# Moving the high and low slices of the activations 32 bytes apart by the remainder of 64

## The chip, the cores and the metric

The kernel runs on one core of a Trainium2 chip. The metric is the device time of one execution in microseconds; the time before is 1422.66 us, the median of three runs (1421.84 to 1422.71). A core has a matrix engine (TensorE, PE in the profile, with PEld for its weight loads), VectorE (DVE), ScalarE (ACT), GpSimd (POOL) and SyncE (SP), which work side by side and wait for each other by semaphores. On-chip memory (SBUF) has 128 partitions; an address in this text is the byte offset within a partition, the same in all of them. Matmul results land in PSUM.

## The reference, cut to what matters

The computation is a chain of transformer-like blocks on one sequence of 256 tokens and 1024 features, in float32.

```python
# first block
xn = rmsnorm(h, norm_mix_g)
q, k, v, xr, gr, ga, gb = split(xn @ w_in)
ya = chunked_band_attention(q, k, v, rel_table) @ w_attn_out
hr = rg_lru(causal_depthwise_conv(xr, conv_w, conv_b), ...)
yb = (hr * gelu(gr)) @ w_rnn_out
h = h + (sigmoid(ga + ...) * ya + sigmoid(gb + ...) * yb) @ w_o
h = h + (silu(g) * up) @ w_ffn_out          # g, up = split(rmsnorm(h) @ w_ffn_in)
x = rmsnorm(h, final_norm_g)
# second block, two layers: half-weighted feed-forward, mixer, half-weighted feed-forward
x = x + 0.5 * swiglu(rms_norm(x), w_in, w_out)      # four of these
x = x + chunked_sgu(h, ...)                          # layer 0: gated unit, v layer-normed
x = x + stick_breaking_attention(q, k_shared, v_shared) @ b_w_o   # layer 1
return rms_norm(x, final_norm)
```

Nearly all of the work is products of the 256 x 1024 activations with weight matrices.

## The kernel before, in words

The activations lie transposed: 128 features on the partitions, 256 tokens along the free dimension, so 1024 features are eight slices with k = 0 to 7. The weights come in as 240 groups of 1 MB (`PLAN`), each of two chunks of 128 x 1024. A chunk is of kind A (one block of 128 output features, all eight k: `pe_a`), K (two k, four output blocks: `pe_k`, or `pe_nat` where the activations are stationary and the weights move), or R (one k, eight output blocks: `pe_r`, and `pe_rn` with the weights moving).

For float32 accuracy each factor is split into a high part, rounded to the type fp32r, and a low part, the rest. `prep` does it for the weights (ScalarE line 163, VectorE line 164). A product is then three matmuls, `mm3` (line 213): weight high with activation high, weight high with activation low, weight low with activation high. The weight is the stationary operand (128 x 128), the activation slice the moving one: 256 columns of 4 bytes, so 1024 bytes per partition. All matmuls go through `mm` (line 211) in the order of the program; nothing reorders them.

The activation slices lie in two places. `self.XS` is a pair of tiles, `xh` and `xl`, of 128 x 8 x 256; it holds the normed input of each stage, written by `split_h` (ScalarE, line 262) and `split_l` (VectorE, line 267), one slice at a time. `self.RR` is four tiles of the same size for what comes between: RR[0] and RR[1] hold the high and low parts of the hidden activations (written by `hl_split`, lines 318 and 319), RR[2] and RR[3] those of the attention; in the gated unit the high parts fill RR[0] and RR[1] and the low ones RR[2] and RR[3].

Between the streams stand a few other matmuls: `stat_mm` sums squares (moving operand one column of `ones`); `bcast_mm` spreads the two columns of reciprocal norms `rc` (or `rckv`, for the keys and values, and `r1c`), stationary, against `ident`; `nudge` is one bf16 matmul of 32 columns on 64 partitions, with `identb` as both operands; the gate products of the recurrent part and those within the two attentions are plain fp32.

Constant tiles are laid one behind the other in the order of their declarations, each taking a multiple of 32 bytes. In `setup` the first is `par` (896 bytes, at 16512), then `x0` to `x3` (17408 on), `xh` (25600), `xl` (33792), `rr0` to `rr3` (41984, 50176, 58368, 66560), `sa`, six slabs, `ident`, `ones`. All of these start at a multiple of 64. The 8 bytes of `mhalf` (133248) put `rt`, `r1t`, `rkv` and `rckv` (136352) at remainder 32 of 64; `rc` is at 136448, remainder 0; `identb` (137696) at remainder 32.

Of the kernel before, what the change touches and what calls it, by code (L numbers as in the profile page):

```python
# [10 lines left out]
F32R = mybir.dt.float32r  # L11
# [90 lines left out]
for _n, _c in PARAMS:  # L102
    OFF[_n] = NPAR
    NPAR += _c


class Builder:
    def __init__(self, tc, dram, pools):
        self.tc, self.nc, self.dram = tc, tc.nc, dram
        self.cp, self.rawp, self.hlp, self.accp, self.wkp = pools  # L110
        self.ci = 0
        self.preps = 0
        self.loads = 0
        self.raw = {}
        self.hl = {}
        self.gens = []
        self.R = None
        self.rcol = None
        self.due = False
# [207 lines left out]
    def setup(self):  # L327
        nc, dram = self.nc, self.dram
        self.P = self.sb("par", [128, 224])[:, 0:NPAR]
        self.X = [self.sb(f"x{p}", [128, 2, 256]) for p in range(4)]  # L330
        self.XS = (self.sb("xh", [128, 8, 256], F32R), self.sb("xl", [128, 8, 256], F32R))
        self.RR = [self.sb(f"rr{i}", [128, 8, 256], F32R) for i in range(4)]
        self.SA = self.sb("sa", [128, 2080])[:, 0:8 * 259]
        self.SL = {c: self.sb("s" + c, [128, 2048]) for c in "bcdfgh"}
        self.ident = self.sb("ident", [128, 128])
        self.ones = self.sb("ones", [128, 128])
        self.mhalf = self.sb("mhalf", [128, 2])
        self.Rt = self.sb("rt", [128, 256])
        self.R1 = self.sb("r1t", [128, 256])
        self.Rkv = self.sb("rkv", [128, 256])  # L340
        self.rckv = self.sb("rckv", [128, 16])[:, 0:2]
        self.v2 = self.sb("v2", [128, 2])
        self.rc = self.sb("rc", [128, 2])
        self.tiny = self.sb("tiny", [128, 1])
        self.c8 = self.sb("c8", [128, 8])
        self.nc8 = self.sb("nc8", [128, 8])
        self.half = self.sb("half", [128, 24])
        self.sq = self.view("b", 4)
        nc.scalar.dma_start(self.P, dram["par"])
        x_load = lambda p: nc.sync.dma_start(self.X[p], dram["x"][:, 2 * p:2 * p + 2, :])  # L350
        for f in range(2):
            nc.sync.dma_start(self.X[0][:, f, :], dram["x"][:, f, :])  # L352
        self.warm_up()
        for g in range(2):
            t = self.rawp.tile([128, 2048], F32, tag="raw", name="raw")
            for c in range(2):
                if 2 * g + c:
                    x_load(2 * g + c)
                n = 512 if 2 * g + c == 0 else 1024
                for o in range(c * 1024, (c + 1) * 1024, n):  # L360
                    nc.sync.dma_start(t[:, o:o + n], dram["w"][g, :, o:o + n])  # L361
            self.raw[g] = t
        self.loads = 2
        self.load()
        self.gw = self.SL["h"].rearrange("p (a b) -> p a b", b=128)
        make_identity(nc, self.ident)
        nc.gpsimd.memset(self.ones, 1.0)
        nc.gpsimd.memset(self.mhalf, -0.5)
        nc.gpsimd.memset(self.tiny, 2.0 ** -115)
# [606 lines left out]
    def sgu(self, fin, fin_l):  # L976
# [6 lines left out]
        tmp = [SA[:, i * 512:(i + 1) * 512].rearrange("p (a b) -> p a b", b=256) for i in range(2)]  # L983
        rs = SL["b"][:, 0:1024]
        bs = SL["b"][:, 1024:2048]
        st6 = self.sb("bn6", [128, 2, 4, 6])
        mv = self.sb("mv", [128, 2, 2])
        rstd = self.sb("rstd", [128, 2])
        nc.gpsimd.dma_start(ws, dram["ws"])
        nc.gpsimd.affine_select(out=ws, in_=ws, pattern=[[0, 8], [1, 128]], compare_op=ALU.is_ge, fill=0.0,  # L990
                                base=0, channel_multiplier=-1)
# [367 lines left out]
```

## Time and profile before

| | before |
|---|---|
| median of three runs | 1422.66 us |
| profiled execution | 1422.0 us |
| its span, first to last instruction | 1420.3 us |
| granted TensorE clock, mean | 0.999 |
| TensorE matmuls, busy | 1410.6 us, 99% |
| TensorE weight loads, busy | 1368.7 us, 96% |
| VectorE, busy | 949.8 us, 67% |
| ScalarE, busy | 735.0 us, 52% |
| DMA | 260.31 MB, mean 183 GB/s |

A matmul's own duration in the profile (about 280 ns for 256 columns) is the time from its start to the modelled end of its results; matmuls overlap, so the distance between two starts is what adds up to the span. Weight loads run beside the matmuls in front of them.

### The profile page before, as it was taken

Reading aid. Unit: us, or ns where it says so; the run is one execution under the profiler, and the core shown is the slowest. Engines: PE = TensorE matmul, PEld = TensorE weight load, DVE = VectorE, ACT = ScalarE, POOL = GpSimd, SP = SyncE. Lnnn points to the kernel's source line nnn. Section 1 sums busy time; section 2 is a strip of 40 time slices with the busy share of each in tenths; the row PEclk is TensorE's granted clock in tenths of the full one; section 3 lists DMA queues with packets and bytes.
Section 4 is the critical chain, followed back from the end, with each engine's and each line's share of the span. In section 5 each row is a group of like instructions: output and inputs, shape, how many; then the busy total and the mean of one; then the engine's idle time right before and its main releaser. Section 6 shows DMA issues by size and latency. Waiting matters only on the chain.

```text
span 1420.3 us, 26991 instructions
## 1 busy us (share of the span) xinstructions
PE 1410.6 (99%) x11564; PEld 1368.7 (96%) x11564; DVE 949.8 (67%) x1316; ACT 735.0 (52%) x1094; POOL 24.7 (2%) x57
## 2 busy tenths in 40 slices
PE   9999999999999999999999999999999999999998
PEld 9998999999999999998999999999999998999997
DVE  6976687665567666677785665667665677656663
ACT  5686465544445445455445444446544477544442
POOL 0000000000000000000000000000000000000000
PEclk9999999999999999999999999999999999999999
DMA  8555554555544555556445554454555552445551
GB/s 299 192 198 197 176 189 154 203 195 191 179 178 149 206 182 206 203 198 223 160 156 183 186 206 179 178 188 169 208 184 211 199 179 90 161 152 197 190 187 51
DMA packets 37624, 260.31 MB, mean 183 GB/s; under 512 B 4224, under 2 KB 4608, under 8 KB 7040
## 3 DMA queue, kind: packets, MB, share of 16 engines
q1 hardware_dynamic: 36288, 253.77, 50.1%
q0 software_dynamic: 1072, 4.72, 1.0%
q8 instruction: 90, 1.47, 0.4%
q14 instruction: 30, 0.25, 0.1%
q10 hardware_dynamic: 144, 0.10, 0.0%
HBM read 257.53 MB, written 1.05 MB: 182 GB/s over the span
## 4 chain that ended last, share of the span: by engine, by line
PE 98%; DMA 0%; ACT 0%; DVE 0%; SPq 0%; issue 0%; POOLq 0%; POOL 0%
PE wk L211 62%; PE acc L211 36%; DMA raw<-w 0%; PE acc L530 0%; PE wk L530 0%; ACT sf L971 0%; ACT sd L961 0%; DVE l L164 0%; ACT h L163 0%; SPq L361 0%; SPq L352 0%; DVE sf L962 0%; POOLq L1355 0%; POOL rc L284 0%; ACT sh L1148 0%
## 5 line engine op out<-in xcount | busy, mean ns | idle before, releaser
L164 DVE TENSOR_TENSOR l<-raw,h 128x1024 fp32r<-128x1024 f32 (+1 forms) x479 | 571.3, 1220 | 241.3 <-ACT h L163 240.9
L211 PE MATMUL wk<-xh,h 128*128 128x256 f32 x2272 | 637.5, 281 | 1.4 <-ACT h L163 1.4
L211 PE MATMUL wk<-xh,l 128*128 128x256 f32 x2272 | 633.5, 279 | 0.1
L211 PE MATMUL wk<-xl,h 128*128 128x256 f32 x2272 | 633.2, 279 | 0.0
L163 ACT ACTIVATE h<-raw 128x1024 fp32r<-128x1024 f32 (+1 forms) x479 | 486.3, 1046 | 61.3 <-PE acc L211 28.0
L211 PEld LDWEIGHTS wk<-xh,h 128*128 128x128 f32 x2272 | 430.8, 190 | 4.5 <-issue 2.0
L211 PEld LDWEIGHTS wk<-xh,l 128*128 128x128 f32 x2272 | 427.7, 188 | 0.5 <-DVE l L164 0.5
L211 PEld LDWEIGHTS wk<-xl,h 128*128 128x128 f32 x2272 | 427.6, 188 | 0.5
L211 PE MATMUL acc<-rr,h 128*128 128x256 f32 x2016 | 353.5, 279 | 0.0
L211 PEld LDWEIGHTS acc<-rr,h 128*128 128x128 f32 x2016 | 306.1, 189 | 2.1 <-issue 1.9
L211 PE MATMUL acc<-rr,l 128*128 128x256 f32 x1008 | 280.4, 278 | 0.0
L211 PEld LDWEIGHTS acc<-rr,l 128*128 128x128 f32 x1008 | 189.3, 188 | 0.0
L748 ACT ACTIVATE sa<-sa 128x256 f32<-128x256 f32 x110 | 45.4, 417 | 258.5 <-DVE sa L315 258.3
L318 ACT ACTIVATE rr<-sa 128x256 fp32r<-128x256 f32 (+1 forms) x122 | 52.7, 439 | 185.3 <-DVE sa L753 128.9
L315 DVE TENSOR_TENSOR sa<-wk,rt 128x512 f32<-128x512 f32 x92 | 62.4, 687 | 72.5 <-PE wk L211 54.8
L319 DVE TENSOR_TENSOR rr<-sa,rr 128x256 fp32r<-128x256 f32 (+1 forms) x122 | 54.1, 451 | 53.4 <-ACT rr L318 53.4
L211 PE MATMUL acc<-h,rr 128*128 128x512 f32 (+1 forms) x208 | 63.1, 374 | 0.0
L211 PEld LDWEIGHTS acc<-h,rr 128*128 128x128 f32 x208 | 38.5, 188 | 6.6
L262 ACT ACTIVATE xh<-x,par 128x256 fp32r<-128x256 f32 x56 | 25.0, 501 | 29.4 <-DVE x L325 16.2
L211 PE MATMUL acc<-l,rr 128*128 128x512 f32 (+1 forms) x104 | 39.0, 375 | 0.0
L753 DVE TENSOR_TENSOR sa<-sa 128x256 f32<-128x256 f32 x88 | 37.1, 429 | 0.0
L211 PE MATMUL wk<-rr,h 128*128 128x256 f32 x192 | 33.0, 277 | 0.0
(255 smaller groups left out, 972.8 us busy)
## 6 DMA issues: line engine op xcount, KB each, us to landing
raw<-w SPq DMA_DIRECT2D x237, 1024.0 KB, 5.0
sd<-bias POOLq DMA_DIRECT2D x8, 384.0 KB, 3.4
raw<-w SPq DMA_DIRECT2D x3, 512.0 KB, 7.6
sh<-gates SPq DMA_DIRECT2D x1, 1024.0 KB, 9.1
out<-sf SPq DMA_DIRECT2D x4, 256.0 KB, 2.2
x<-x SPq DMA_DIRECT2D x3, 256.0 KB, 6.6
raw<-w SPq DMA_DIRECT2D x2, 256.0 KB, 4.9
sa<-ws POOLq DMA_DIRECT2D x1, 512.0 KB, 3.8
```

Of the source, the lines that this page charges most:

```text
L163: nc.scalar.activation(h[:, s], raw[:, s], AF.Copy)
L164: nc.vector.tensor_tensor(l[:, s], raw[:, s], h[:, s].bitcast(F32), op=ALU.subtract)
L211: self.nc.tensor.matmul(out, lhsT, rhs, start=start, stop=stop, skip_group_check=True)
L262: self.nc.scalar.activation(xs[0][:, k, :], src[p][:, f, :], AF.Copy, scale=self.par(*g(k)))
L315: self.nc.vector.tensor_tensor(dst, bank, self.Rpair(), op=ALU.mult)
L318: self.nc.scalar.activation(zh, src, AF.Copy)
L319: self.nc.vector.tensor_tensor(zl, src, zh.bitcast(F32), op=ALU.subtract)
L748: nc.scalar.activation(t[:, 0, :], t[:, 0, :], AF.Silu)
L753: nc.vector.tensor_tensor(t[:, 1, :], t[:, 0, :], t[:, 1, :], op=ALU.mult)
```

## The change: two tiles become four, and small tiles move between them

The two tiles `xh` and `xl` of eight slices are each cut into two tiles of four slices, one for even k and one for odd k. A small class, `Slices`, lets the code index them as before. Small constant tiles that stood further down (or in `sgu`) are declared between the large ones, so that the large ones behind them start 32 bytes off a multiple of 64 or on one again. By the declarations, the remainders of 64 after are: `xh0` 0, `xh1` 32, `xl0` 32, `xl1` 0; `rr0` 0, `rr1` 32, `rr2` 32, `rr3` 0. `rt`, `r1t`, `rkv`, `rckv` and `identb` come to remainder 0, `rc` stays at 0. The weights' tiles are not moved.

```diff
+class Slices:
+    def __init__(self, aps):
+        self.aps = aps
+    def __getitem__(self, i):
+        return self.aps[i[1]][i[0], i[2]]
...
-        self.XS = (self.sb("xh", [128, 8, 256], F32R), self.sb("xl", [128, 8, 256], F32R))
-        self.RR = [self.sb(f"rr{i}", [128, 8, 256], F32R) for i in range(4)]
+        quarter = lambda n: self.sb(n, [128, 4, 256], F32R)
+        xh0 = quarter("xh0")
+        self.rc = self.sb("rc", [128, 2])
+        xh1, xl0 = quarter("xh1"), quarter("xl0")
+        self.half = self.sb("half", [128, 24])
+        self.c8, self.nc8 = self.sb("c8", [128, 8]), self.sb("nc8", [128, 8])
+        self.mhalf = self.sb("mhalf", [128, 2])
+        self.v2 = self.sb("v2", [128, 2])
+        xl1 = quarter("xl1")
+        self.XS = tuple(Slices([t[k % 2][:, k // 2, :] for k in range(8)]) for t in ((xh0, xh1), (xl0, xl1)))
+        tile8 = lambda i: self.sb(f"rr{i}", [128, 8, 256], F32R)
+        self.RR = [tile8(0)]
+        self.tiny = self.sb("tiny", [128, 1])
+        self.RR += [tile8(1), tile8(2)]
+        self.bn6 = self.sb("bn6", [128, 2, 4, 6])
+        self.rstd = self.sb("rstd", [128, 2])
+        self.RR.append(tile8(3))
...
-        st6 = self.sb("bn6", [128, 2, 4, 6])
+        st6 = self.bn6
-        rstd = self.sb("rstd", [128, 2])
+        rstd = self.rstd
```

## Rows read from the trace of the kernel before

**Rows 1.** The page: span, busy time of each engine, granted clock in 40 slices.
```profile
span 1420.3 us, 26991 instructions
...
PE 1410.6 (99%) x11564; PEld 1368.7 (96%) x11564; DVE 949.8 (67%) x1316; ACT 735.0 (52%) x1094; POOL 24.7 (2%) x57
...
PEclk9999999999999999999999999999999999999999
```

**Rows 2.** The page: chain that ended last, by engine and by line.
```profile
PE 98%; DMA 0%; ACT 0%; DVE 0%; SPq 0%; issue 0%; POOLq 0%; POOL 0%
```

**Rows 3.** Groups of instructions: operands and count | busy us, mean ns | idle before.
```profile
L211 PE MATMUL wk<-xh,h 128*128 128x256 f32 x2272 | 637.5, 281 | 1.4 <-ACT h L163 1.4
L211 PE MATMUL wk<-xh,l 128*128 128x256 f32 x2272 | 633.5, 279 | 0.1
L211 PE MATMUL wk<-xl,h 128*128 128x256 f32 x2272 | 633.2, 279 | 0.0
L164 DVE TENSOR_TENSOR l<-raw,h 128x1024 fp32r<-128x1024 f32 (+1 forms) x479 | 571.3, 1220 | 241.3 <-ACT h L163 240.9
...
L211 PE MATMUL acc<-rr,h 128*128 128x256 f32 x2016 | 353.5, 279 | 0.0
...
L211 PE MATMUL acc<-rr,l 128*128 128x256 f32 x1008 | 280.4, 278 | 0.0
...
L319 DVE TENSOR_TENSOR rr<-sa,rr 128x256 fp32r<-128x256 f32 (+1 forms) x122 | 54.1, 451 | 53.4 <-ACT rr L318 53.4
...
L262 ACT ACTIVATE xh<-x,par 128x256 fp32r<-128x256 f32 x56 | 25.0, 501 | 29.4 <-DVE x L325 16.2 <-DVE x L323 12.1 <-DMA par<-par 1.1
L267 DVE SCALAR_TENSOR_TENSOR xl<-x,par,xh 128x256 fp32r<-128x256 f32 x56 | 23.8, 479 | 1.4 <-ACT xh L262 1.4
```

**Rows 4.** Chain that ended last, in order of time: start us, us, what.
```profile
274.24 5.76 PE wk L211 x48
280.56 8.69 PE wk L211 x72
...
842.47 11.31 PE wk L211 x96
...
975.67 5.76 PE wk L211 x48
981.99 8.38 PE wk L211 x72
...
1028.78 10.88 PE wk L211 x96
```

**Rows 5.** Windows, TensorE alone: window, length, busy (count), clock, DMA share, GB/s.
```profile
297.00:461.00 164.00, 164.00 (x1395) 1.00 0.50 180
809.00:975.00 166.00, 166.00 (x1412) 1.00 0.53 190
...
484.00:630.00 146.00, 146.00 (x1291) 1.00 0.59 212
...
997.00:1130.00 133.00, 133.00 (x1176) 1.00 0.56 197
...
108.00:126.00 18.00, 18.00 (x79) 1.00 0.52 177
```

**Rows 6.** Group of the gate matmuls (first line); timeline at 46 and 1277 us.
```profile
L211 PE MATMUL acc<-sb,sh 128*128 128x256 f32 x32 | 7.6, 379 | 0.0
...
46.45 1.89 PE L211 MATMUL acc<-sb,sh 128*128 128x256 f32 x8
...
1276.89 0.39 PE L211 MATMUL acc<-l,rr 128*128 128x512 f32 x1
1277.12 0.62 PE L211 MATMUL acc<-h,rr 128*128 128x512 f32 x2
1277.57 0.39 PE L211 MATMUL acc<-l,rr 128*128 128x512 f32 x1
```

**Rows 7.** Timeline of TensorE near 280 and 981 us: where the norms are spread.
```profile
279.83 0.61 PE L211 MATMUL acc<-ident,rc 128*128 128x128 f32 x4
280.37 0.19 PE L211 MATMUL acc<-identb 64*128 64x32 bf16 x1
...
981.26 0.61 PE L211 MATMUL acc<-ident,rckv 128*128 128x128 f32 x4
981.80 0.19 PE L211 MATMUL acc<-identb 64*128 64x32 bf16 x1
```

More of the change, by code (lines that the diff above doesn't have):

```diff
@@ L336, in setup @@
         self.ones = self.sb("ones", [128, 128])
-        self.mhalf = self.sb("mhalf", [128, 2])
         self.Rt = self.sb("rt", [128, 256])
@@ L341, in setup @@
         self.rckv = self.sb("rckv", [128, 16])[:, 0:2]
[L342 to L347, printed above, removed]
         self.sq = self.view("b", 4)
```

## The prediction

> **What bounds the kernel now.** I read the summary first. TensorE's matmuls cover 1410.6 of 1420.3 us with a granted clock of nine tenths or more in all 40 slices, while VectorE is busy 67% and ScalarE 52% [rows 1]. A busy TensorE may only be a pipelined one, so the chain of waits comes next: 98% of it is TensorE's own queue at line 211, DMA and the other engines together stay at a few tenths of a per cent [rows 2]. The table of waits and idle times agrees: the largest group of matmuls has 1.4 us of idle time before it, the others 0.1 or none [rows 3]. So the time is the number of matmuls times the distance from one start to the next, and only that distance matters.
>
> What is that distance? In the chain, a piece of 96 matmuls of 256 columns takes 11.31 us at 842.47 and 10.88 us at 1028.78 [rows 4]: 117.8 ns and 113.3 ns a step, for the same shapes and the same code. The windows, with a granted clock of 1.00 in each, show that this is no local noise: 297 to 461 us holds 1395 matmuls (117.6 ns each) and 809 to 975 holds 1412 (117.6), while 484 to 630 holds 1291 (113.1) and 997 to 1130 holds 1176 (113.1) [rows 5]; a window counts the one or two that only reach into it. I call the two the long and the short step. One lasts for more than a hundred microseconds and changes only near matmuls of another shape. Taking the start-to-start distance of all 256-column fp32r matmuls in the trace, 5,646 lie between 112 and 114 ns (mean 113.32) and 4,685 between 116 and 120 (mean 117.78): 639.8 + 551.8 = 1191.6 us, 84% of the span. The same number follows within a few matmuls from the counts by operand: 3 x 2272, 2016 and 1008 [rows 3], and some 480 in smaller groups.
>
> [...]
>
> **The change part by part.** It removes and adds no instruction, DMA or wait. It moves addresses. Each constant tile takes a multiple of 32 bytes; before, every fp32r moving operand starts at remainder 0 of 64. After: the high slices of even k start at 0, of odd k at 32, the low ones the other way round; of the four rr tiles, 0 and 3 stand at 0, 1 and 2 at 32. The order is (weight high, x high), (weight high, x low), (weight low, x high), and so on.
>
> *How many successive moving operands differ.* The plan has 268 "A" chunks of 24 matmuls that walk through k: all 6,432 steps alternate. Of 40 "K" chunks, 24 read the quartered slices; 18 of 24 steps alternate for the first three k-pairs and all 24 for the last: 468 of 576. The other 16 read rr tiles, which don't change with k: 16 of 24, so 256. The 120 "R" chunks with 256 columns read rr tiles, high-low-high for each of eight outputs, so 16 of 24: 1,920. The key/value chunks give 32. Together 9,108 of about 10,320.
>
> *What a step then costs.* [...] One pair of places bears on it. Near 280 us and near 981 us the same thing happens: 48 matmuls at the long step behind the statistics (5.76 us each time), four matmuls that spread the column of reciprocal norms, a bf16 matmul, and the stream goes on. After the first, 72 matmuls take 8.69 us; after the second, 8.38 us, and the long step has turned into the short one [rows 4, 7]. The four matmuls take 0.61 us both times. By the declarations they differ in the place of their stationary operand: `rc` lies at remainder 0, `rckv` at 32. So a shift of 32 bytes in one small operand can go with the end of the long step, which then doesn't return for some 100 us. It isn't the only cause: other entries with `rc` end short as well. A pattern that repeats the same remainder for each operand can hold the long step; I expect that one in which the remainder changes at 88% of the steps can't. The nearest row is therefore the short step of the same instruction, 113.3 ns, and I take it for all 10,331: 4,685 x (117.78 - 113.32) = 20.9 us less. I take nothing from below 113.3, since no row has an fp32r matmul of this shape there.
>
> *Stationary operands.* In the value projections, the first projection of the gated block and the last output projection the slices are the stationary operand, with 552 matmuls of 512 columns. The weights that they stream don't move. Their start distances go from 230 and 225 ns (from 1276.89 to 1277.12, and half of the way to 1277.57 [rows 6]) to 234 (18 us for 77 whole ones between 108 and 126 us [rows 5]); 8 ns either way on all are 4.4 us, and I take 0.
>
> *Writers.* The 56 scalings on ScalarE (501 ns) and 56 on VectorE (479 ns), and the 122 low parts (451 ns), write to the shifted tiles [rows 3]. They lie beside the matmuls, on engines that are idle a third to a half of the time; 10% more on each would be 13 us of VectorE or ScalarE work, all hidden but the few last pieces at the stage borders (under 1 us). The row tile of the norms moves from remainder 32 to 0; the same cover holds. With TensorE 1.5% faster, what is late next would be the weight preparation, VectorE's 479 splits of 1220 ns; it waits 241 us for ScalarE's half, and there TensorE waits 1.4 us in all [rows 3], so 21 us of less cover are absorbed. The small matmuls that stand between the streams lose the 32 bytes of `identb` and `rckv`; that may start a stage in the other step, and the range holds it.
>
> Sum: the span falls from 1420.3 to 1399.4 us. The profiled execution took 1422.0, 1.7 us more than its span, and the median is 0.66 us above that execution: 1401.8, so 1402 us.
>
> **Rivals.** [...]
>
> *The shift does nothing.* The reading may go in pieces that divide 32 bytes; then each operand costs the same pieces at either start, and the two steps stay where they are: 1423 us. For it: both steps occur with every operand at remainder 0, so something else can make them. Against it: [rows 4, 7], as above. [...]
>
> *The long step everywhere.* The shifted operand starts in the middle of a 64-byte piece and ends in one. If the matmul behind it then waits for the rest of its reading, as a stream at the long step seems to, alternation holds the whole kernel at 117.8: 5,646 x 4.46 = 25.2 us more, 1448 us. For it: nothing in the trace ties the short step to a remainder, and 45% of the matmuls are long already with a regular pattern. Against it: [rows 4, 7]. It decides from 45% long steps on (4,685 of 10,331); above that the kernel is slower than before.
>
> **How the numbers follow.** Chances: forecast 0.36, columns 0.20, nothing 0.16, long step 0.28. A measurement of this kernel tells about 0.2% (2.8 us) from no change. Faster: 0.36 + 0.20 + 0.02 of the third, in which small matmuls start some stage in the other step; within 0.2%: 0.12; slower: 0.28 + 0.02. The range reaches from the columns rival, some microseconds below it for the steps that I left at 113.3, to the long step: 1358 to 1448. The forecast's own range, with the 4.4 us of the 512-column matmuls and one stage of some 1,400 matmuls (6 us) in the long step, is 1393 to 1412.
>
> **What would show it.** Right: in the chain every piece of 96 takes 10.88 us, those at 313 to 460 and 820 to 970 us too, and no window of a feed-forward stage has a step near 117. [...] Nothing: the windows of [rows 5] with the same counts. Long step: 11.31 us everywhere. I am wrong in kind if steps appear that are neither 109, 113 nor 118 ns, if odd and even k differ, or if TensorE waits for VectorE or ScalarE for more than the 1.4 us of before.

## The result and the profile after

The kernel after takes 1455.03 us (median of four runs, 1454.91 to 1455.10) against 1422.62 before: a ratio of 1.0228, with a 95% interval from 1.0215 to 1.0241. It is slower by 32.4 us, where 1402 us was forecast, and lies 7 us above the range.

The page of the kernel after, as [rows 1 and 2], and its two largest groups of matmuls, with the writers of the slices, as [rows 3] (line numbers are those of the new file):

```profile
span 1453.2 us, 26991 instructions
...
PE 1443.2 (99%) x11564; PEld 1400.4 (96%) x11564; DVE 950.5 (65%) x1316; ACT 735.1 (51%) x1094; POOL 24.9 (2%) x57
...
PEclk9999999999999999999999999999999999999999
...
PE 99%; DMA 0%; ACT 0%; issue 0%; DVE 0%; SPq 0%; POOLq 0%; POOL 0%
...
L220 PE MATMUL wk<-xh,h 128*128 128x256 f32 x2272 | 642.4, 283 | 1.8 <-ACT h L172 1.8
L220 PE MATMUL wk<-xl,h 128*128 128x256 f32 x2272 | 638.2, 281 | 0.0
...
L328 DVE TENSOR_TENSOR rr<-sa,rr 128x256 fp32r<-128x256 f32 (+1 forms) x122 | 54.1, 450 | 53.4 <-ACT rr L327 53.4
L271 ACT ACTIVATE xh<-x,par 128x256 fp32r<-128x256 f32 x56 | 25.3, 502 | 32.3 <-DVE x L334 18.0
```

The same number of instructions, the same bound, the same clock; the writers to the shifted tiles take what they took (450 against 451 ns, 502 against 501). TensorE waits as little as before. So the loss must be in the step, and the chain in order of time shows it (start us, us, what), as [rows 4]:

```profile
279.78 5.79 PE wk L220 x48
286.13 8.72 PE wk L220 x72
...
843.51 11.36 PE wk L220 x96
854.87 5.71 PE acc L220 x48
...
994.65 5.79 PE wk L220 x48
1001.01 8.71 PE wk L220 x72
...
1032.81 11.36 PE wk L220 x96
```

and so do windows of TensorE in the four feed-forward stages, as [rows 5] (window, length, busy, matmuls, clock, DMA share, GB/s):

```profile
302.00:466.00 164.00, 164.00 (x1386) 1.00 0.51 182
827.00:992.00 165.00, 165.00 (x1394) 1.00 0.52 186
492.00:638.00 146.00, 146.00 (x1234) 1.00 0.57 205
1016.00:1150.00 134.00, 134.00 (x1133) 1.00 0.53 190
```

All four have the same mean step now: 118.3 to 118.4 ns. No stage has one of the two steps of before. A `wk` piece of 96 takes 11.36 or 11.37 us everywhere, above the 11.31 of the long step [rows 4], and the entry near 1001 us, after which 72 matmuls took 8.38 us before, takes 8.71. The start times show that this is no third constant. In an A chunk the distances repeat after twelve matmuls, to 1 ns: 117, 121, 116, 119, 117, 121, 117, 119, 116, 121, 117, 119 ns. In an R chunk they repeat after six: 117, 121, 116, 120, 124, 114.

The mean over all 256-column fp32r steps is 118.49 ns instead of 115.38 (counted where one such matmul follows another, without the distances of 200 ns and more, at which a record is missing or TensorE waited), and for 512 columns 231.1 instead of 229.35. That is 10,331 x 3.11 = 32.1 us and 552 x 1.75 = 1.0 us, together 33.1 of the span's 32.9. The step accounts for all of the loss; the question is what sets the step.

### The profile page after: what moved, and what is told of

Its sections match the earlier page's. It is cut to its first block, busy times and chain, and to the rows that moved or that the text cites. A ratio compares the mean times of both kernels' runs of the same rounds, so it can differ in the third digit from the quotient of the medians.

```text
span 1453.2 us, 26991 instructions
## 1 busy us (share of the span) xinstructions
PE 1443.2 (99%) x11564; PEld 1400.4 (96%) x11564; DVE 950.5 (65%) x1316; ACT 735.1 (51%) x1094; POOL 24.9 (2%) x57
## 4 chain that ended last, share of the span: by engine, by line
PE 99%; DMA 0%; ACT 0%; issue 0%; DVE 0%; SPq 0%; POOLq 0%; POOL 0%
PE wk L220 62%; PE acc L220 36%; DMA raw<-w 0%; PE acc L549 0%; PE wk L549 0%; ACT sf L990 0%; ACT sd L980 0%; SPq L371 0%; DVE sf L981 0%; ACT h L172 0%; POOLq L1374 0%; POOL rc L293 0%; ACT sh L1167 0%; DVE v L985 0%; POOLq L293 0%
## 5 line engine op out<-in xcount | busy, mean ns | idle before, releaser
L220 PE MATMUL acc<-rr,h 128*128 128x256 f32 x2016 | 363.8, 283 | 0.0
```

What stands on the lines that cost most here:

```text
L220: self.nc.tensor.matmul(out, lhsT, rhs, start=start, stop=stop, skip_group_check=True)
```

## The experiments

### Back to remainder 0 of 64: e1

The small tiles between the large ones are padded to 64 bytes; everything else is as after.

```diff
-        self.rc = self.sb("rc", [128, 2])
+        pad = lambda n, w: self.sb(n, [128, -(-w // 16) * 16])[:, 0:w]
+        self.rc = pad("rc", 2)
...
-        self.tiny = self.sb("tiny", [128, 1])
+        self.tiny = pad("tiny", 1)
```

> The kernel after with every small tile between the large ones padded to 64 bytes, so that all moving slices are back at remainder 0; the four slice tiles, the moved small tiles and the other addresses (row tiles of the norms, identb, rckv at remainder 0) stay as after. Theory 'mixing' (the price is paid where successive moving operands have different remainders) and theory 'straddle' (each operand at remainder 32 pays for itself) both expect two steps of 113.3 and 117.8 ns again and 1402 to 1448 us. Rival 'small tiles' (the cut of the slice tiles or the moved small tiles made the loss): 1455 us with steps of 118.5.

Measured: 1449.11 us (ratio 1.0186, interval 1.0171 to 1.0201). The loss stays, and yet it isn't the step of after: the mean is 117.94 ns, and distances go from 112 to 131. The chain shows pieces that fit neither of the two steps of before:

```profile
310.49 5.81 PE acc L220 x48
316.30 11.22 PE wk L220 x96
327.52 5.81 PE acc L220 x48
333.34 11.22 PE wk L220 x96
```

96 in 11.22 us are 116.9 ns, 48 in 5.81 are 121.0. Theories 'mixing' and 'straddle' expected two steps and got neither; the rival 'small tiles' had the time nearly right and the steps wrong. What I had overlooked is in the addresses: `xh0` at 25600, `xh1` 29760, `xl0` 33856, `xl1` 38336 and `rr0` 42432 are all multiples of 64, but by the remainder of 256 they lie at 0, 64, 64, 192 and 192. Before, all of them were at 0 there too. Counted from the weights, which start at 64 past a multiple of 256, e1 has slices 192, 0 and 128 bytes behind, and before has 192 throughout. So e1 was no way back, and it was the first sign that more than the remainder of 64 counts.

### All moving slices at remainder 32: e2

```diff
-        xh0 = quarter("xh0")
         self.rc = self.sb("rc", [128, 2])
-        xh1, xl0 = quarter("xh1"), quarter("xl0")
...
+        xh0, xh1, xl0, xl1 = quarter("xh0"), quarter("xh1"), quarter("xl0"), quarter("xl1")
...
+        self.RR = [tile8(i) for i in range(4)]
```

with the other small tiles behind.

> The kernel after with all moving slices at remainder 32: high and low slices of all k and the four rr tiles. Successive moving operands have the same remainder again, but every one is shifted. 'Mixing': steps of 113.3 and 117.8 ns, 1402 to 1448 us. 'Straddle': after has half of its operands shifted and lost 5.2 ns a step against 113.3, so all of them lose 10.4: 123.7 ns a step, about 1508 us. A third theory, 'relation to the weights' (what counts is how the moving operand lies to the stationary one, which stays at 0): one step in the whole kernel that is neither, between 113 and 124 ns, and no return of the two steps.

Measured: 1453.89 us (ratio 1.0219, interval 1.0202 to 1.0236); one mean step in the whole kernel, 118.31 ns. Two of its feed-forward stages, one that was long before and one that was short, as [rows 5]:

```profile
302.00:466.00 164.00, 164.00 (x1388) 1.00 0.51 182
...
492.00:638.00 146.00, 146.00 (x1236) 1.00 0.57 205
```

Both have 118.1 to 118.2 ns. Here successive moving operands have equal remainders, and the time is that of after less 1.1 us. So the alternation, which the change is about, is not what costs: a shift of all slices by 32 costs the same. 'Mixing' falls, as it asked for the old steps; 'straddle' falls, as it asked for 1508 us. Of the three theories the relation to the weights is left; they lie at 64 past a multiple of 256 in before, after, e1 and e2 alike.

### The step by itself: e3 and e5

A kernel of matmuls alone: weights and slices are loaded and rounded once, then each setting of the offsets runs 96 matmuls in the order of an A chunk, behind a gap of about 1 us. `mslice` and `wslice` take the offset in bytes into the tile as their last argument.

```python
a, b = (lo, hi) if flip and k % 2 else (hi, lo)
xh, xl = mslice("xh", k, a), mslice("xl", k, b)
wh, wl = wslice("h", k, w), wslice("l", k, w)
mm(out, wh, xh, k == 0, False)
mm(out, wh, xl, False, False)
mm(out, wl, xh, False, k == 7)
```

> A kernel that computes nothing of the reference (its output is zeros): 18 settings of the remainders, each with 96 fp32r matmuls of 256 columns in the order of an A chunk, entered twice (behind a gap; behind a gap, one fp32 matmul of one column and one bf16 matmul of 32 columns). Settings are (high, low, change places with odd k, weights) in bytes. (0,0,no,0): 113.3 or 117.8 ns by the entry. (0,32,yes,0): 118.5 in both entries. 'Mixing': (32,32,no,0) as (0,0,no,0), (0,32,no,0) and (32,0,no,0) between it and 118.5, the weights' 32 bytes change nothing. 'Straddle': (32,32,no,0) 123.7, (0,32,no,0) 117 (one shifted of three), (32,0,no,0) 120 (two of three). 'Relation to the weights': (32,32,no,32) as (0,0,no,0), (0,0,no,32) as (32,32,no,0), and (0,32,yes,32) about as (0,32,yes,0). If pieces of 64 bytes matter, (64,64,no,0) and (0,64,yes,0) are as (0,0,no,0); 16 bytes show whether 32 is the size.

A setting is named (high slices, low slices, whether the two change places with odd k, weights). All tiles of e3, e5 and e8 begin 128 past a multiple of 256 (the first at 16512, each a multiple of 256 long), and offsets count from there. The windows of e3 run from the first start of a setting to the last, 95 steps of which the first, from the small matmuls or the gap, is longer. In order: (0,0,no,0), (32,32,no,0), (0,0,no,32), (32,32,no,32), (64,64,no,0) in its two entries, (0,0,no,64):

```profile
25.05:36.54 11.49, 11.49 (x96) 1.00 0.00 0
50.58:61.76 11.18, 11.18 (x95) 1.00 0.01 1
...
150.91:162.25 11.34, 11.34 (x95) 1.00 0.01 1
176.15:187.65 11.50, 11.50 (x95) 1.00 0.00 0
...
378.75:390.04 11.29, 11.29 (x95) 1.00 0.01 2
391.54:402.41 10.87, 10.87 (x96) 1.00 0.00 0
403.47:414.36 10.89, 10.89 (x96) 1.00 0.01 2
```

Three things are to be seen. Slices and weights at the same place, (0,0,no,0), have 120.0 ns, almost without change from one distance to the next, where I had expected 113.3 or 117.8. Shifting both by 32 gives the same 11.50 us; shifting either alone does not. And with a distance of 64 between them there are two steps, 117.8 and 113.3, by the entry: the pair of before. Shifts of the slices by 8 bytes, and of low and high slices in turn by 256, also give 120.0, so from distance 0 neither changed the step. One expectation of 'relation to the weights' failed: the weights moved by 32 have 118.3 ns, the slices moved by 32 have 116.7, so it counts which of the two lies behind.

e5 walks through the remainder of 256 in steps of 16.

> A kernel that computes nothing of the reference (output zeros): steps of fp32r matmuls for moving operands 0, 16, ... 240 bytes past a multiple of 256 with the weights at a multiple of 256, each entered in three ways; then the remainders of the kernels (weights at 64; slices at 0, at 32, and at 0 and 32 in turn); then 512 columns with the roles changed. 'Relation to the weights' expects by what e3 showed: 0: 120.0, 16: 118.7, 32: 116.7, 48: 118.3, 64: 113.3 or 117.8, 192: 113.3, 224: 118.3, 240: 118.3; (0,0) with weights at 64 as 192; (32,32) with weights at 64 as 224, 118.3, the step of e2; in turn: 118.5, the step of after. If the relation counts by the remainder of 128, then 128 to 240 repeat 0 to 112; if by 256, 128 is a value of its own. A rival in which the place of the moving operand alone counts expects (0,0) with weights at 64 to give 120.0.

Settled mean steps in ns, by how far the slices lie behind the weights (one number: the same in all three entries):

| distance (bytes) | step (ns) | distance (bytes) | step (ns) |
|---|---|---|---|
| 0 | 120.0 | 128 | 118.6 |
| 16 | 116.7, 118.7, 113.3 | 144 | 118.6 to 118.8 |
| 32 | 116.7, 117.8, 116.7 | 160 | 117.3, 117.3, 118.6 |
| 48 | 118.3 | 176 | 119.3 |
| 64 | 117.8, 113.3, 117.8 | 192 | 113.3, 117.8, 117.8 |
| 80 | 120.0 | 208 | 119.2 |
| 96 | 120.0 | 224 | 118.3 |
| 112 | 113.3 | 240 | 117.2 |

The expected 118.3 at 240 and the single 113.3 at 192 did not come. The table is not one value per distance either, and the entry alone doesn't choose among several. With the slices moved to 16, e3 had 118.7 ns in both entries, where e5, with the same addresses and the same two entries, had 116.7 and 118.7. At 240, e3 had 118.3 in both of its entries, by weights moved 16, and e5 117.2 in its three, by slices moved 240.

The kernel before has slices at 0 and weights at 64: distance 192. Its setting rebuilt, (0,0) with weights at 64, in the first and third entry, then slices at 0 and 32 in turn, then all at 32:

```profile
718.50:729.79 11.29, 11.29 (x95) 1.00 0.00 0
744.56:755.44 10.88, 10.88 (x99) 1.00 0.01 2
679.93:691.27 11.34, 11.34 (x95) 1.00 0.00 1
756.50:767.84 11.34, 11.34 (x96) 1.00 0.01 1
```

Two steps for before, 113.3 in another entry than at 192 in the table; one step of 118.3 for e2's distance of 224; and 118.3 for after, in all entries. With nothing but matmuls, and 128 bytes further along, the sweep gives the steps of the three kernels. The rival in which the moving operand's place alone counts falls, and 128 to 240 don't repeat 0 to 112 (118.6 ns at 128, 120.0 at 0), so the relation counts by 256 and not by 128.

### Slices back at multiples of 256, and the weights moved alone: e4 and e6

e4 is after with its small tiles gathered behind the large ones; e6 adds the last line below, a pad that moves the weights and the buffers that they are loaded into, and nothing else.

```diff
+        xh0, xh1, xl0, xl1 = quarter("xh0"), quarter("xh1"), quarter("xl0"), quarter("xl1")
...
+        self.RR = [tile8(i) for i in range(4)]
         self.rc = self.sb("rc", [128, 2])
...
         self.half = self.sb("half", [128, 24])
...
         self.ss = self.sb("ss", [128, 2, 2])
+        self.sb("endpad", [128, 48])
```

> The kernel after with its small tiles gathered behind the large ones, so that all slice tiles start at a multiple of 256 again, as before, while the cut of the slice tiles and the places of all tiles behind them (row tiles, ident, identb, rckv) stay as after. The weight tiles start at 64 past a multiple of 256 in both kernels. Theory now: the step depends on how the moving operand lies to the stationary one by the remainder of 256 (e1 had slices at 0, 64 and 192, so it was no way back). It expects the two steps of before, 113.3 and 117.8, in shares that the small tiles may change: 1400 to 1448 us, no step of 115, 120 or 131. Rival 'small tiles': 1449 us with the steps of e1 (112 to 131).

> e4 with a pad of 192 bytes behind the last constant tile, which puts the weight tiles at a multiple of 256, as the slices; no slice is moved. 'Relation to the weights': 120.0 ns in each 256-column step, as (0,0,no,0) of e3: 10,331 x 120.0 = 1239.7 instead of 1191.6 us, so about 1471 us. 'Remainder of the moving operand alone' (64 or 256): as e4, 1400 to 1448 us.

Measured: e4 1427.08 us (ratio 1.0032, interval 1.0020 to 1.0044), e6 1467.18 us (1.0313, interval 1.0295 to 1.0330). The chain of e4 near 500, 984 and 1034 us:

```profile
494.40 5.65 PE acc L220 x48
500.06 11.31 PE wk L220 x96
...
980.81 5.76 PE wk L220 x48
987.13 8.38 PE wk L220 x72
...
1033.92 10.88 PE wk L220 x96
```

11.31 and 10.88 are back, the pieces of before. The cut of the tiles and the moved small tiles together cost 4.4 us. What changed is which step a stage has: 4,403 distances are at most 115 ns instead of 5,570 before, and the stage at 500 us is long now and was short before. In e6 no slice moved and each step went to that of the setting in which slices and weights lie alike:

```profile
851.05 11.52 PE wk L220 x96
862.57 5.76 PE acc L220 x48
```

96 in 11.52 us are 120.0 ns; the mean is 119.94, and 10,331 x (119.94 - 115.38) = 47.1 us, less 1.3 for the 512-column matmuls (227.07 ns), is 45.8 of the span's 45.5. A pad of 192 bytes that no instruction reads cost 40 us against e4. By itself e6 would leave open that the place of the weights alone counts. e3 closes that: weights moved by 32 have 120.0 ns when the slices move with them and 118.3 when they don't.

### A distance of 112, and what pairs: e7 and e8

112 is the one distance with the short step in every entry. e7 puts the slices of before there. `xs` begins at 25760 and `rr` at 42400, both 160 past a multiple of 256, and the slices 16 bytes further; a pad keeps the weights at 64:

```diff
+        cut = lambda t, i: t[:, 4 + i * 2048:4 + (i + 1) * 2048].rearrange("p (a b) -> p a b", b=256)
+        xs = self.sb("xs", [128, 2 * 2048 + 8], F32R)
+        self.XS = (cut(xs, 0), cut(xs, 1))
...
+        rr = self.sb("rr", [128, 4 * 2048 + 8], F32R)
+        self.RR = [cut(rr, i) for i in range(4)]
```

> The kernel of before's slices in two long tiles, each begun 16 bytes into its tile, so that every moving slice starts at 176 past a multiple of 256 and the weights, by a pad behind the constants, at 64 as before: the moving operand lies 112 behind the stationary one, the only setting of the sweep that gave 113.3 ns in all three entries. 'Relation to the weights' expects one step, 113.3 to 113.5, in all 256-column streams: 1191.6 - 10,331 x 113.4 = 20.1 us less; the 552 matmuls with 512 columns come to about 233.8 instead of 229.4 (2.4 us more); in sum about 1405 us and no piece of 96 over 10.95 us. If the sweep doesn't carry over (the streams of the kernel lock by something else), two steps stay, or one that is longer: 1423 us or more.

Measured: 1407.26 us (1406.92 to 1407.44), ratio 0.9892 to before (interval 0.9875 to 0.9908): 1.1% below before and clear of the noise. Its chain in the first and third feed-forward stage, both long before:

```profile
272.38 5.56 PE wk L220 x48
278.50 8.41 PE wk L220 x72
...
325.35 10.88 PE wk L220 x96
...
847.65 10.88 PE wk L220 x96
858.53 5.44 PE acc L220 x48
```

The mean step is 113.70 ns, 17.4 us less in 10,331; the 512-column matmuls have 233.1 ns, 2.1 us more; 15.3 of the span's 14.6 us. It is 2 us above the 1405 expected: some 640 steps, behind the borders between matmuls of different shapes, are longer than 115 ns until the stream settles.

> A kernel that computes nothing of the reference (output zeros): settings (high, low moving; high, low weights), 48 matmuls each behind a gap. While a matmul streams, the weights of the next one load; so the pairs that run together are high slice with high weight (two of three) and low slice with low weight (one). If only these pairs count, (112, 0; 0, 144) has 112 in all pairs and steps of 113.3 as (112, 112; 0, 0), while (0, 112; 144, 0), with 112 in the two other combinations and other values in these pairs, is longer, 116 to 120. If a matmul's own weights count instead, it is the settings with high-high, high-low and low-high at 112 alone that are short, which only (112, 112; 0, 0) and (176, 176; 64, 64) are. 140 drawn settings then show whether any step is below 113.3; no theory of mine expects one.

That the weights of the next matmul load while one streams is in the trace of before: the load for the matmul of 500.19 us starts at 500.08, together with the matmul in front of it, and takes 0.19 us.

Measured: (112, 112; 0, 0), (112, 0; 0, 144) and (176, 176; 64, 64), 47 steps each:

```profile
26.06:31.54 5.48, 5.48 (x47) 1.00 0.00 0
46.06:51.70 5.64, 5.64 (x48) 1.00 0.00 0
72.99:78.44 5.45, 5.45 (x47) 1.00 0.02 3
```

The three have 113.3, 117.8 and 113.3 ns once settled. The second should have been short, for its high slices lie 112 behind the high weights and its low ones 112 behind the low weights; so the theory that only those pairs count falls. The rival, a matmul's own weights, isn't shown either: the drawn setting (144, 96; 0, 32), with its high slice 144 and 112 behind the two weights and its low one 96 behind, has 113.3 as well. Among 140 drawn settings that is the only one below 115 ns, none is below 113.3, the mean is 118.2. Each setting had one entry only. Which pair of operands sets the step stays open.

## Why the prediction was wrong, point by point

*What bounds the kernel* was right. The time is matmuls times step: the sums shown above for after, e6 and e7 give their spans within 1 us.

*No instruction added, writers hidden, TensorE's waits* were right: 1.8 us of waits, writers unchanged. *Stationary operands*: taken as 0 with 4.4 us either way, measured 1.0 more.

*The small matmuls that may start a stage in the other step* stood in the range, with one stage and 6 us, and not in the sum. In e4 they come, with the cut of the tiles, to 4.4 us.

*What a step then costs* is the step that failed. Its term, 20.9 us less, came out as 32.1 us more. It had three faults. First, it asked how successive moving operands lie to each other. e2 has all of them alike and e6 moves none of them from e4; both change the time, so what counts is how they lie to the weights. The text noted that the weights aren't moved and didn't see that this is just what changes the relation. Second, the nearest row was taken as the value: 113.3 ns, a step that belongs to certain distances (112 always, 16, 64 and 192 sometimes in the sweep) and not to the instruction. The distances of after, 192 and 224 in turn, have 118.3 to 118.5. Third, the pair of places in [rows 4, 7] was read as a sign that 32 bytes of a small stationary operand end the long step. e4 has `rckv` at a multiple of 64 and shows the same 8.38 us for the 72 matmuls behind it. So the remainder of 64 isn't the cause of the turn, and the cause stays open; by the remainder of 256 `rc` and `rckv` still lie apart in e4, at 0 and 128, which no run tests.

*The upper end of the range* was the long step. But 117.8 ns is the upper one of two steps at one distance, and no bound over distances: the sweep has 120.0, and e6 ran the kernel there. That is why the measured time lies above the range.

*Columns*, with its 0.20, its 109 ns and the lower end of the range at 1358 us, stands on a step that no run shows: no setting tried has a step below 113.3 ns. What the runs show of columns is a difference: at distance 0 in e5, 512 columns have 226.7 ns and 256 have 120.0, so that 256 more columns add 106.7 ns there.

*Slips in the working*, none of which turns the result: the counts 5,646 and 4,685 hold some 190 distances at matmuls of other shapes (between fp32r matmuls of 256 columns alone they are 5,553 and 4,592, and the gain would be 20.5 us); 10% on the writers is 11 us and not 13; and 4.4 us less than 1402 is 1398, so that nothing in the text gives the 1393 of the forecast's own range.

*The rivals.* The long step everywhere, 1448 us, was nearest in time and right that the shift would hold the whole kernel above the mean of before. That nearness is luck, for its mechanism, a shifted operand that waits for the rest of a 64-byte piece, is not what the runs show: in e3 slices shifted with their weights cost what unshifted ones cost. "The shift does nothing" is out by 32 us, and its premise, that an operand costs the same at either start, is not what was measured: e2, with every slice 32 bytes on, takes 31 us more than before. From distance 0, 8 bytes leave the step at 120.0 ns (e3), and 16 bring it to 113.3, 116.7 or 118.7 (e5).

Moving the weights alone takes the steps of 113.3 and 117.8 ns to 120.0 (e4 and e6), so the place of the stationary operand bears on the step. Whether it is the loading of the next weights that slows the running matmul, no run shows.

*Left open*: why some distances have several steps, what chooses one, and why the distance between the operands counts at all. The runs show that it does, not by what mechanism.

## What to carry to other kernels

Where a kernel is bound by a stream of fp32r matmuls, look at the distance between starts and not at busy time, and at the remainder of 256 by which moving and stationary operands lie apart; between the best and the worst padding tried here (e7 with 1407.26 us and e6 with 1467.18) lie 4%. A layout change of that kind should be undone and redone with all addresses written out, as a pad that keeps one remainder (64 in e1) may change another. Sweep the disputed cost by itself before laying out the kernel: one run of matmuls alone gave the setting that took 1.1% off.

## What was not expected of the hardware

The step of fp32r matmuls with 256 columns depends on the distance between moving and stationary operand, by the remainder of 256 (113.3 ns at 112 and 120.0 at 0 in e5). From distance 0, 8 bytes changed nothing (e3: 120.0 ns) and 16 did (e3: 118.7). It takes values such as 113.3, 116.7, 117.8, 118.3 and 120.0 ns in e5. That nothing else in the addresses counts isn't shown: at 240, e3 has 118.3 ns and e5 117.2. No setting went below 113.3 ns. At 192 two steps each last for over 100 us (before and e4), and in the sweep 16, 32, 64, 160 and 192 have more than one, by the entry and by something that wasn't found. For 512 columns the same relation gives 226.7 ns at distance 0, where 256 columns have their longest step, 228.9 at 64, and 232 to 234 at the other distances tried.
